# Four parts of layer 1's modulation computed beside layer 0's latent MLP, and two key weights split in the code ahead of a norm

## The chip, the cores and the metric

The kernel runs on one core of a Trainium2 chip. TensorE (PE in the profile) multiplies matrices, and its loads of stationary operands are listed as PEld; VectorE is DVE, ScalarE is ACT, GpSimd is POOL, and SP issues most of the DMAs. The metric is the device time of one launch in microseconds (us), the median of several runs.

## The reference

A backbone of two layers over 512 latent tokens and 256 context tokens, width 1024. Layer 0 mixes with mLSTM and RWKV heads, layer 1 with RG-LRU and neighbourhood attention; `ox` and `oc` below are the mixers' outputs. Each layer normalises, modulates, mixes, adds through a gate, and then does the same around a squared-ReLU MLP of width 4096. Shift, scale and gate of both halves of a layer are six vectors of 1024, the layer's *modulation*; they come from the conditioning vectors alone, so that they can be computed at any time before they are used.

```python
def ada_modulation(cond, w, b):
    m = jax.nn.silu(cond) @ w + b
    return jnp.split(m[:, None, :], 6, axis=-1)
...
    for layer in range(DEPTH):
        last = layer == DEPTH - 1
        sx1, cx1, gx1, sx2, cx2, gx2 = ada_modulation(c, ada_w[layer], ada_b[layer])
        sc1, cc1, gc1, sc2, cc2, gc2 = ada_modulation(c_ctx[None], ada_w[layer], ada_b[layer])
        nx = modulate(rms_norm(h_lat), sx1, cx1)
        nc = modulate(rms_norm(h_ctx), sc1, cc1)
...
        h_lat = h_lat + gx1 * ox
        h_lat = h_lat + gx2 * sq_relu_mlp(modulate(rms_norm(h_lat), sx2, cx2), mlp_w1[layer], mlp_w2[layer])
        if not last:
            h_ctx = h_ctx + gc1 * oc
            h_ctx = h_ctx + gc2 * sq_relu_mlp(modulate(rms_norm(h_ctx), sc2, cc2), mlp_w1[layer], mlp_w2[layer])
    return rms_norm(h_lat) * final_norm_w
```

## The kernel before

All matrix products go through the helper `mm` (L134), so most matmuls carry that line, and tiles tell them apart: `psg` is the output of a dense product, `psada` that of a modulation product. A scheduler under the program models each engine, and from the order in which the code asks for things and from its own costs it fixes the order of the instructions on each engine before the run. Every engine then works its own row in that order and waits at the first instruction whose operand is not there.

**A dense product** (`gemm`, L239) loads one weight block `w` by a DMA on SP, casts it on ScalarE to a rounded half `wh` (L232), subtracts it on VectorE or GpSimd to get the rest `wl` (L236), and runs 24 matmuls. `split_w` is the first part alone, `gemm_w` the second. After each product `gemm` adds a rate to a counter, and whenever the counter reaches one it takes one step of a *background* generator:

```python
        bg[2] += bg[1]
        while bg[2] >= 1.0:
            bg[2] -= 1.0
            next(bg[0], None)
```

**The background** is `ada` (L158), the modulation. One layer has six parts. A part is two *loads* of 2 MB (two DMAs of 1 MB each) into the one buffer `adaw` of its pool; each load feeds 16 program matmuls of 256 columns, which the trace lists as 32 records. After the second load come a copy to `rows` (L172), two transposes (L175) and four small VectorE instructions that write `mod` (L184). With one `adaw` buffer, a load is issued only after the matmuls of the load before it.

**Stages in time.** Up to about 355 us ("the heads stage") the kernel works off a string of letters (L1083): digits are steps of the four mLSTM heads of the context, `c` is a step of the RWKV input projection of the context, `a` starts the background, `R` ends the projection, drains the background and runs `pre(0, X)`, the preparation of the first RWKV step. `pre` stores a matrix to memory (`bkD`, L799), loads it back in another layout (L844), and the first RWKV matmul is `psA`. At the end of a head, the normalised head `hall` is made on GpSimd (L663, L673) and transposed by TensorE (L678); the RWKV projection has its own chain of small products (`psb`, `psw`, `psv`) for which VectorE, ScalarE and GpSimd work in turn. Up to about 985 us follow twelve RWKV steps with *fillers* (other work of layer 0) pulled between them by a table of counts; then the output projection of the latent tokens, and from about 1000 to 1366 us layer 0's latent MLP: four chunks, each of eight products into the hidden width and eight back, 64 in all, with `psg` of 128x512. Beside it run the background and, once, the norm of the context for layer 1 (`norm_mod` into `xhc`, `xlc`), which needs the shift and the scale, the first two parts of layer 1's modulation. Then come the norm of the latent tokens for layer 1 (`norm_mod(res, ...)`, whose last ScalarE step before the broadcast is `rs` at L310), the twelve key and value products of the context (`ukv`), and the rest of layer 1.

Of the kernel before, what the change touches and what calls it, by code (L numbers as in the profile page):

```python
# [21 lines left out]
CT = 256  # L22
# [95 lines left out]
def hybrid_kernel(ctx: ExitStack, tc: tile.TileContext, A, out):  # L118
    WS = [int(x) for x in "2222"]
    nc = tc.nc  # L120
# [37 lines left out]
    def ada(layer, parts, pa, psa, tag):  # L158
        for pair, half in parts:
            ps = psa.tile([P, 256], F32, tag=tag, name=nm("psada"))  # L160
            for k0 in range(0, NK, 4):

                w = pa.tile([P, 4, D], F32, tag="adaw", name=nm("adaw"))
                for i in range(0, 4, 2):
                    nc.sync.dma_start(w[:, i:i + 2, :], A["ada_w"][layer, pair, half, (k0 + i) // 2])
                for i in range(4):
                    k = k0 + i
                    for j in range(4):
                        mm(ps[32 * j:32 * j + 32, :], sc[:, k, :], w[:, i, 256 * j:256 * j + 256], k == 0, k == NK - 1)
                yield 1.8  # L170
            rows = pa.tile([P, 256], F32, tag="rows", name=nm("rows"), bufs=1)
            nc.vector.tensor_copy(rows, ps)  # L172
            pt = psa.tile([P, 2, P], F32, tag=tag, name=nm("pst"))
            for t in range(2):
                nc.tensor.transpose(pt[:, t, :], rows[:, P * t:P * t + P], ident)  # L175
            src = pt.rearrange("p t (i j r) -> p i t j r", i=2, j=2)
            for i, idx in enumerate(PAIRS[pair]):
                o = 8 * idx + 4 * half
                dst = mod[:, layer, o:o + 4, :].rearrange("p (j t) c -> p t j c", t=2)
                bo = COLS["ada_b"][0] + 48 * layer + o  # L180
                bias = cols[:, bo:bo + 4].rearrange("p (j t) -> p t j", t=2)
                one = 1.0 if idx in (1, 4) else 0.0
                for cnd in range(2):
                    nc.vector.scalar_tensor_tensor(dst[:, :, :, cnd], src[:, i, :, :, cnd], one, bias, op0=ALU.add, op1=ALU.add)  # L184
# [35 lines left out]
    bg = [iter(()), 0.0, 0.0]  # L220
# [18 lines left out]
    def gemm(ap, xs, psp, both=0, k0=0, k1=NK, x0=0):  # L239

        w = split_w(ap[:, P * k0:P * k1], both)
        res = [gemm_w(w, x, psp, x0) for x in xs]
# [4 lines that stand above are left out]
        return res  # L247
# [168 lines left out]
    psa1 = st_p1.enter_context(tc.tile_pool(name="psa1", bufs=1, space=PSUM, side="right"))  # L416
# [4 lines left out]
    with tc.tile_pool(name="pn", bufs=2) as pn, tc.tile_pool(name="pa0", bufs=16) as pa0:  # L421
# [11 lines left out]
        for q in range(4):  # L433
            ada_first(q, pa0, psa1, "ada")
            if q == 0:
                ws = [split_w(A["ev_in"][i], 2, pn) for i in range(2)]
# [33 lines left out]
    pa1 = st_a.enter_context(tc.tile_pool(name="pa1", bufs=1))  # L470
# [611 lines left out]
    work["c"] = rwkv_in(0, psg2, psm, "m")  # L1082
    for o in "0000a0c1ccc1cc11c1c22cc2c23c12ccc33cR33":  # L1083
        if o == "a":
            bg[:] = [itertools.chain(ada(0, ((1, 0), (1, 1), (2, 0), (2, 1)), pa1, psa1, "ada"),
                                     ada(1, ((0, 0), (0, 1), (1, 0), (1, 1)), pa1, psa1, "ada")), 0.5, 0.0]
        elif o == "R":
            for _ in itertools.chain(work["c"], bg[0]):
                pass
            bg[1] = 0  # L1090
            st_a.close()
            YA[0] = st_y.enter_context(tc.tile_pool(name="py", bufs=1)).tile([P, 4, 4, 64], F32, name="ya_c")
            pr = st_r.enter_context(tc.tile_pool(name="pr", bufs=1))
            add_set()
            banks.update(A=(psh2, "h", 1), I=(psa1, "ada", 1))
            S = sets[0].tile([P, 2, 4, 64], F32, tag="S", name="S0")
            nc.vector.memset(S, 0.0)
            X = new_x(0)
            nc.vector.memset(X[0:64], 0.0)
            pre(0, X)  # L1100
        else:
            next(work[o], None)
# [46 lines left out]
    ukv = plat.tile([P, 3, 4, CT], F32, name="ukv")  # L1149
# [3 lines left out]
    xhc = px1c.tile([P, NK, CT], F32R, name="xh1c")  # L1153
# [15 lines left out]
            pass  # L1169
        rb = stats.rms()  # L1170
    pa3 = st_3.enter_context(tc.tile_pool(name="pa3", bufs=1))
    bg[:] = [ada(1, ((2, 0), (2, 1)), pa3, psa3, "ada"), 0.25, 0.0]
    stats = Stats(LT, None, psa3, "st")
    for j, _ in enumerate(mlp(0, 0, LT, res, 8, psg3, "right", 0, rb, 2, stats)):
        if j == 8:
            with tc.tile_pool(name="pn1c", bufs=2) as pn:
                norm_mod(RES["c"], CT, 1, 1, 0, xhc, xlc, pn, stats_of(RES["c"], CT, pn, psg3).rms())
    for _ in bg[0]:
# [7 lines left out]
    xh = px.tile([P, NK, LT], F32R, name="xh1")  # L1186
    xl = px.tile([P, NK, LT], F32R, name="xl1")
    XL = [(xh, xl, LT)]
    with tc.tile_pool(name="pn1", bufs=2) as pn:
        norm_mod(res, LT, 0, 1, 0, xh, xl, pn, stats.rms(psg3, "g", work=pn))  # L1190
    for j, t0 in enumerate((0, 12, 16)):
        for i in range(4):
            ps, = gemm(A["od_in"][t0 + i], [(xhc, xlc, CT)], psg3, 2)
            nc.scalar.copy(ukv[:, j, i, :], ps)
    st_3.close()

    st_1 = ExitStack()
# [279 lines left out]
```

## Time and profile before

| | |
|---|---|
| time, median of 3 runs | 2068.69 us (2068.35 to 2078.05) |
| the profiled execution: its time | 2068.99 us |
| its span in the trace | 2067.1 us (1.9 us lie around it) |
| its mean granted TensorE clock | 0.971 of full speed |
| TensorE busy | 1959.7 us (95%) |
| VectorE, ScalarE, GpSimd busy | 1086.7 us (53%), 874.4 us (42%), 835.1 us (40%) |
| moved by DMA | 271.62 MB, 131 GB/s over the span |

TensorE is busy almost throughout, but its share is an average over stages: near full in the MLP and in most of the heads stage, lower at the end of the heads stage and in the RWKV steps. What an edit is worth therefore depends on the stage in which it takes or adds work.

### The profile page before, as it was taken

Reading aid. Unit: us, or ns where it says so; the run is one execution under the profiler, and the core shown is the slowest. Engines: PE = TensorE matmul, PEld = TensorE weight load, DVE = VectorE, ACT = ScalarE, POOL = GpSimd, SP = SyncE. Lnnn points to the kernel's source line nnn. Section 1 sums busy time; section 2 is a strip of 40 time slices with the busy share of each in tenths; the row PEclk is TensorE's granted clock in tenths of the full one; section 3 lists DMA queues with packets and bytes.
Section 4 is the critical chain, followed back from the end, with each engine's and each line's share of the span. In section 5 each row is a group of like instructions: output and inputs, shape, how many; then the busy total and the mean of one; then the engine's idle time right before and its main releaser. Section 6 shows DMA issues by size and latency. Waiting matters only on the chain. (4 is left out here: it accounts for less than half of the span.)

```text
span 2067.1 us, 36765 instructions
## 1 busy us (share of the span) xinstructions
PE 1959.7 (95%) x14924; PEld 1601.4 (77%) x14924; DVE 1086.7 (53%) x2087; ACT 874.4 (42%) x1441; POOL 835.1 (40%) x561
## 2 busy tenths in 40 slices
PE   6899999898887999999999999999999999999998
PEld 4788876776676899888787888887666687888887
DVE  6764555677878667766632221363656663122122
ACT  5444444354534444443433232343665743233232
POOL 1455554233432222224343444434545544444444
PEclk9999998898998999999999999999999999999999
DMA  8355557454585455553524232344120123322232
GB/s 322 96 202 207 192 207 246 107 153 108 165 247 156 123 172 158 149 138 123 209 97 133 92 100 94 94 127 127 51 62 29 59 67 93 100 92 92 93 98 74
DMA packets 171833, 271.62 MB, mean 131 GB/s; under 512 B 74960, under 2 KB 113488, under 8 KB 166544
## 3 DMA queue, kind: packets, MB, share of 16 engines
q1 hardware_dynamic: 166608, 263.76, 40.9%
q10 hardware_dynamic: 5056, 5.51, 0.8%
q8 instruction: 118, 1.93, 0.4%
q14 instruction: 51, 0.42, 0.1%
HBM read 244.06 MB, written 25.17 MB: 130 GB/s over the span
## 5 line engine op out<-in xcount | busy, mean ns | idle before, releaser
L236 POOL TENSOR_TENSOR wl<-w,wh 128x1024 fp32r<-128x1024 f32 (+3 forms) x252 | 573.5, 2279 | 861.0 <-PE psg L134 434.7
L232 ACT CAST wh<-w 128x1024 fp32r<-128x1024 f32 (+3 forms) x319 | 313.4, 985 | 529.0 <-PE psg L134 449.3
L134 PE MATMUL psg<-xh,wh 128*128 128x512 f32 (+1 forms) x1440 | 499.6, 362 | 13.6 <-DVE tm L884 6.1
L134 PE MATMUL psg<-xl,wh 128*128 128x512 f32 (+1 forms) x1440 | 498.9, 359 | 0.7 <-DVE xl L330 0.3
L134 PEld LDWEIGHTS psg<-xh,wh 128*128 128x128 f32 x1440 | 272.6, 191 | 69.6 <-issue 20.1
L134 PE MATMUL psg<-xh,wl 128*128 128x512 f32 (+1 forms) x1440 | 326.4, 357 | 0.0
L134 PEld LDWEIGHTS psg<-xl,wh 128*128 128x128 f32 x1440 | 274.6, 191 | 48.0 <-issue 7.4
L134 PEld LDWEIGHTS psg<-xh,wl 128*128 128x128 f32 x1440 | 242.1, 191 | 43.1 <-issue 7.0
L134 PE MATMUL psg<-hl,wh 128*128 128x512 f32 (+1 forms) x800 | 269.4, 351 | 0.9 <-DVE hl L276 0.9
L134 PE MATMUL psg<-hh,wh 128*128 128x512 f32 (+1 forms) x800 | 267.0, 350 | 0.6 <-DVE res_c L333 0.4
L333 DVE SCALAR_TENSOR_TENSOR res_l<-psg,mod,res_l 128x512 f32<-128x512 f32 (+1 forms) x108 | 74.1, 689 | 281.7 <-PE psg L134 281.7
L134 PEld LDWEIGHTS psg<-hl,wh 128*128 128x128 f32 x800 | 151.2, 189 | 22.5 <-DVE hl L276 1.3
L134 PEld LDWEIGHTS psg<-hh,wh 128*128 128x128 f32 x800 | 150.9, 189 | 22.7 <-issue 0.8
L134 PE MATMUL psg<-hh,wl 128*128 128x512 f32 (+1 forms) x800 | 166.1, 349 | 0.0
L378 DVE TENSOR_SCALAR r<-psg 128x512 f32<-128x512 f32 (+1 forms) x96 | 57.4, 600 | 179.2 <-PE psg L134 179.1
L134 PEld LDWEIGHTS psg<-hh,wl 128*128 128x128 f32 x800 | 131.6, 189 | 20.4
L276 DVE TENSOR_TENSOR hl<-r,hh 128x512 fp32r<-128x512 f32 (+1 forms) x96 | 90.7, 948 | 83.6 <-ACT hh L275 83.4
L379 ACT ACTIVATE r<-r 128x512 f32<-128x512 f32 (+1 forms) x96 | 53.5, 559 | 119.6 <-DVE r L378 119.5
L236 DVE TENSOR_TENSOR wl<-w,wh 128x1024 fp32r<-128x1024 f32 (+1 forms) x67 | 82.1, 1225 | 20.4 <-ACT wh L232 12.7
L884 DVE TENSOR_TENSOR tm<-M,Xi 64x15 f32<-64x15 f32 (+4 forms) x180 | 60.2, 335 | 23.9 <-DMA M<-dA 17.5
L134 PE MATMUL psada<-adaw,sc 128*32 128x256 f32 (+1 forms) x896 | 62.1, 381 | 9.0 <-DMA adaw<-in_ada_w_dram 5.1
L134 PE MATMUL psA<-ar,bk 64*128 64x128 f32 x384 | 55.8, 313 | 6.0 <-issue 3.1
(418 smaller groups left out, 2873.9 us busy)
## 6 DMA issues: line engine op xcount, KB each, us to landing
w<-in_w_dram SPq DMA_DIRECT2D x192, 512.0 KB, 3.6
adaw<-in_ada_w_dram SPq DMA_DIRECT2D x40, 1024.0 KB, 7.4
w<-in_ev_in_dram SPq DMA_DIRECT2D x47, 512.0 KB, 3.7
w<-in_od_in_dram SPq DMA_DIRECT2D x32, 512.0 KB, 3.6
adaw<-in_ada_dram SPq DMA_DIRECT2D x16, 512.0 KB, 11.3
w<-in_out_w_dram SPq DMA_DIRECT2D x32, 256.0 KB, 3.1
bk<-bkD SPq DMA_DIRECT2D x12, 512.0 KB, 4.0
ar<-arD SPq DMA_DIRECT2D x12, 512.0 KB, 5.0
```

What stands on the lines that cost most here:

```text
L134: return nc.tensor.matmul(o, l, r, start=start, stop=stop, skip_group_check=shared, **kw)
L232: nc.scalar.copy(wh, w)
L236: eng.tensor_tensor(wl, w, wh.bitcast(F32), op=ALU.subtract)
L276: nc.vector.tensor_tensor(l, x, h.bitcast(F32), op=ALU.subtract)
L333: nc.vector.scalar_tensor_tensor(r_, ps, modcol(layer, idx, m, cnd), r_, op0=ALU.mult, op1=ALU.add)
L378: nc.vector.tensor_scalar(r_, ps, 0.0, None, op0=ALU.max)
L379: nc.scalar.activation(r_, r_, AF.Square)
L884: nc.vector.tensor_tensor(t_, M[:, m:16, j:j + 1].to_broadcast([64, n, m]), Xi[:, j:j + 1, 0:m].to_broadcast([64, n, m]), op=ALU.mult)
```

## The change

Three places. In the heads stage the background holds only the last four parts of layer 0, at a rate of 0.34 steps a product instead of 0.5; the first four parts of layer 1, which followed there, are gone from it. Beside layer 0's latent MLP the background holds all six parts of layer 1 at 0.34 instead of the last two at 0.25, and the context norm of layer 1 comes after the 25th product rather than the 9th. The first two key weights of the context are split (`split_w`) in the code ahead of the latent norm instead of behind it. The number of modulation products is the same in total.

```diff
     for o in "0000a0c1ccc1cc11c1c22cc2c23c12ccc33cR33":
         if o == "a":
-            bg[:] = [itertools.chain(ada(0, ((1, 0), (1, 1), (2, 0), (2, 1)), pa1, psa1, "ada"),
-                                     ada(1, ((0, 0), (0, 1), (1, 0), (1, 1)), pa1, psa1, "ada")), 0.5, 0.0]
+            bg[:] = [ada(0, ((1, 0), (1, 1), (2, 0), (2, 1)), pa1, psa1, "ada"), 0.34, 0.0]
...
-    bg[:] = [ada(1, ((2, 0), (2, 1)), pa3, psa3, "ada"), 0.25, 0.0]
+    bg[:] = [ada(1, ((0, 0), (0, 1), (1, 0), (1, 1), (2, 0), (2, 1)), pa3, psa3, "ada"), 0.34, 0.0]
     stats = Stats(LT, None, psa3, "st")
     for j, _ in enumerate(mlp(0, 0, LT, res, 8, psg3, "right", 0, rb, 2, stats)):
-        if j == 8:
+        if j == 24:
             with tc.tile_pool(name="pn1c", bufs=2) as pn:
                 norm_mod(RES["c"], CT, 1, 1, 0, xhc, xlc, pn, stats_of(RES["c"], CT, pn, psg3).rms())
...
+    kv_c = [(j, i, t0 + i) for j, t0 in enumerate((0, 12, 16)) for i in range(4)]
+    ws = [split_w(A["od_in"][t], 2) for _, _, t in kv_c[:2]]
     with tc.tile_pool(name="pn1", bufs=2) as pn:
         norm_mod(res, LT, 0, 1, 0, xh, xl, pn, stats.rms(psg3, "g", work=pn))
-    for j, t0 in enumerate((0, 12, 16)):
-        for i in range(4):
-            ps, = gemm(A["od_in"][t0 + i], [(xhc, xlc, CT)], psg3, 2)
-            nc.scalar.copy(ukv[:, j, i, :], ps)
+    for n_, (j, i, t) in enumerate(kv_c):
+        ps = gemm_w(ws[n_], (xhc, xlc, CT), psg3) if n_ < len(ws) else gemm(A["od_in"][t], [(xhc, xlc, CT)], psg3, 2)[0]
+        nc.scalar.copy(ukv[:, j, i, :], ps)
```

What this does to the order on the engines is shown at three places. First TensorE at the end of the third mLSTM head, before: a context product `psg` ends there, then come the transposes of a modulation part, half a modulation load, the transposes of `hall` and the small RWKV products, with a second load between them.

```order
1052 L134 MATMUL psg_3369<-xh_89,wl_3367 128x256 x8
1053 L175 MATMUL pst_3438<-cst,rows_3436 128x128 x2
1054 L134 MATMUL psada_3445<-adaw_3446,sc 32x256 x16
1055 L678 MATMUL pst_2943<-cst,hall_2924 128x128 x2
1056 L678 MATMUL pst_2947<-cst,hall_2924 128x128 x4
1057 L134 MATMUL psb_3012<-q_3009,cst 128x256
```

```order
1064 L802 MATMUL psv_3123<-cst,v_2688 128x128 x2
1065 L134 MATMUL psg_3130<-sgd_1139,gup_2683 128x256
1066 L134 MATMUL psada_3445<-adaw_3557,sc 32x256 x8
1067 L134 MATMUL psw_3073<-low_1144,ul_3070 128x256
1068 L134 MATMUL psw_3078<-low_1146,ul_3070 128x256
1069 L134 MATMUL psada_3445<-adaw_3557,sc 32x256 x8
1070 L134 MATMUL psg_3411<-xh_89,wh_3407 128x256
```

The same place with the change: the head's last `psn` products now stand directly ahead of the transposes of `hall`, with only the two transposes of a modulation part between.

```order
1037 L134 MATMUL psg_3273<-xh_89,wl_3271 128x256 x8
1038 L134 MATMUL psn_2830<-vt_725,e_2711 128x129
...
1043 L134 MATMUL psn_2842<-cn_2835,kq_2150 128x129
1044 L175 MATMUL pst_3434<-cst,rows_3432 128x128 x2
1045 L678 MATMUL pst_2866<-cst,hall_2847 128x128 x2
1046 L678 MATMUL pst_2870<-cst,hall_2847 128x128 x4
1047 L134 MATMUL psb_2916<-q_2913,cst 128x256
```

The context product that stood behind the last `psn` stands ahead of it now, and both modulation loads are gone from between the small products.

Second TensorE in the latent MLP, between two products into the hidden width of its second chunk, before:

```order
3523 L134 MATMUL psg_12892<-xh_12036,wh_12888 128x512
3524 L134 MATMUL psg_12892<-xl_12037,wh_12888 128x512
3525 L134 MATMUL psg_12892<-xh_12036,wl_12890 128x512 x8
3526 L134 MATMUL psg_12928<-xh_12036,wh_12924 128x512
3527 L134 MATMUL psg_12928<-xl_12037,wh_12924 128x512
```

and with the change, where a whole load of the modulation stands between the products:

```order
3511 L134 MATMUL psg_12659<-xh_11844,wh_12655 128x512
3512 L134 MATMUL psg_12659<-xl_11845,wh_12655 128x512
3513 L134 MATMUL psg_12659<-xh_11844,wl_12657 128x512 x8
3514 L134 MATMUL psada_12556<-adaw_12684,sc 32x256 x16
3515 L134 MATMUL psg_12714<-xh_11844,wh_12710 128x512
```

Twelve such loads now lie in the MLP, where there were four.

Third ScalarE around the latent norm of layer 1, before (the casts of the first two key weights are those of `wh_14509` and `wh_14541`; `rs` is the norm's own step):

```order
971 L232 CAST wh_14509<-w_14507 128x1024
972 L298 ACTIVATE sq_14408<-res_l 128x512
973 L232 CAST wh_14541<-w_14539 128x1024
974 L298 ACTIVATE sq_14443<-res_l 128x512
975 L310 ACTIVATE rs_14466<-psst_12028,epsc 128x4
```

and with the change:

```order
968 L232 CAST wh_14465<-w_14463 128x1024
969 L298 ACTIVATE sq_14408<-res_l 128x512
970 L232 CAST wh_14471<-w_14469 128x1024
971 L298 ACTIVATE sq_14443<-res_l 128x512
972 L310 ACTIVATE rs_14478<-psst_11836,epsc 128x4
```

Only the numbers of the tiles differ: the two casts stood ahead of the norm's step before the change too.

## Rows read from the trace of the kernel before

**Rows 1.** The profile page: TensorE's busy tenths and granted clock in 40 equal slices.

```profile
PE   6899999898887999999999999999999999999998
...
PEclk9999998898998999999999999999999999999999
```

**Rows 2.** Windows by stage: start:end, length, busy us (records) of PE, PEld, DVE, ACT, POOL, granted clock.

```profile
100.00:300.00 200.00, 199.22 (x1487) 163.15 (x1491) 108.64 (x238) 85.64 (x172) 109.88 (x93) 1.00 0.57 199
...
310.00:320.00 10.00, 7.29 (x33) 4.76 (x34) 2.66 (x6) 3.32 (x7) 3.46 (x4) 0.54 0.69 230
320.00:330.00 10.00, 10.00 (x79) 6.89 (x79) 8.11 (x22) 7.11 (x17) 6.39 (x11) 0.78 0.98 324
...
420.00:680.00 260.00, 226.78 (x2725) 181.84 (x2724) 201.69 (x452) 121.16 (x223) 88.14 (x82) 0.89 0.58 162
...
1120.00:1360.00 240.00, 240.00 (x1061) 198.72 (x1060) 62.43 (x75) 77.64 (x94) 105.68 (x44) 1.00 0.31 97
```

**Rows 3.** Timeline of PE in the MLP: one burst of half a load, and the next product.

```profile
1015.52 1.07 PE L134 MATMUL psada<-adaw,sc 128*32 128x256 f32 x16
1016.52 0.74 PE L134 MATMUL psg<-xh,wh 128*128 128x512 f32 x2
```

**Rows 4.** Windows of the MLP, instructions on psg alone: with a load, without one.

```profile
1080.00:1100.00 20.00, 18.22 (x81) 14.77 (x80) 2.25 (x3) 0.00 (x0) 1.00 0.51 184
...
1120.00:1140.00 20.00, 20.00 (x89) 16.28 (x88) 2.77 (x4) 0.00 (x0) 1.00 0.27 79
```

**Rows 5.** Tile psada, 1000 to 1200 us: TensorE's idle time before it.

```profile
  issue: 2.8, 9
```

**Rows 6.** Tile adaw in the same stretch: its transfers.

```profile
DMA to landing us min/median/max: 5.0/6.1/7.2
```

**Rows 7.** Timeline of PE at the third head's end; idle before and releaser in brackets.

```profile
302.19 0.39 PE L134 MATMUL psn<-cn,kq 128*128 128x129 f32 x2
...
303.07 0.39 PE L134 MATMUL psg<-xh,wh 128*128 128x256 f32 x1
...
306.05 0.38 PE L175 MATMUL pst<-cst,rows 128*128 128x128 f32 x2
308.75 1.07 PE L134 MATMUL psada<-adaw,sc 128*32 128x256 f32 x16 [2.32 <-DMA adaw<-in_ada_w_dram]
311.91 1.93 PE L134 MATMUL psada<-adaw,sc 128*32 128x256 f32 x16 [2.08 <-DMA adaw<-in_ada_w_dram]
313.77 1.54 PE L678 MATMUL pst<-cst,hall 128*128 128x128 f32 x6
...
320.72 1.94 PE L134 MATMUL psada<-adaw,sc 128*32 128x256 f32 x16
...
324.87 0.39 PE L134 MATMUL psg<-xh,wh 128*128 128x256 f32 x1
```

**Rows 8.** Timeline of POOL there: the last step of `hall`.

```profile
310.16 1.47 POOL L673 TENSOR_TENSOR hall<-hall,rn 128x768 f32<-128x768 f32 x1 [0.58 <-DVE rn L672]
```

**Rows 9.** Timeline of SP's DMA issues during pre(0).

```profile
351.20 0.38 SPq L799 DMA_DIRECT2D bkD<-bk  x1
356.76 0.34 SPq L230 DMA_DIRECT2D w<-in_ev_in_dram  x1
358.61 0.33 SPq L844 DMA_DIRECT2D bk<-bkD  x1
```

**Rows 10.** Tile bkD, 300 to 400 us: its transfers.

```profile
DMA to landing us min/median/max: 3.7/3.9/4.2
```

**Rows 11.** Timeline of PE: the first RWKV matmul.

```profile
365.71 2.05 PE L134 MATMUL psA<-ar,bk 64*128 64x128 f32 x8 [3.09 <-issue]
```

**Rows 12.** Waits of PE, 355 to 1010 us: us in total, times, longest.

```profile
PE psI L134 <- DMA Xr<-invD: 7.3, 5, 3.9
PE psg L134 <- DVE tm L884: 6.1, 2, 4.4
```

**Rows 13.** Timeline of ACT around the latent norm of layer 1.

```profile
1363.91 1.05 ACT L232 CAST wh<-w 128x1024 fp32r<-128x1024 f32 x1 [2.19 <-PE psg L134]
...
1368.30 0.26 ACT L310 ACTIVATE rs<-psst,epsc 128x4 f32<-128x4 f32 x1 [1.14 <-PE psst L134]
```

**Rows 14.** Timeline of PE in the key and value products.

```profile
1399.76 0.58 PE L134 MATMUL psg<-xh1c,wh 128*128 128x256 f32 x1 [3.38 <-ACT wh L232]
```

## The prediction

> **What bounds the kernel now.** I read the page first: TensorE is near full in most slices, with a thinner patch from the eighth to the thirteenth, about 360 to 670 us [rows 1]. A share over the whole span prices no edit, so the windows by stage come next [rows 2]. In the heads stage, 100 to 300 us, TensorE is busy 199.2 of 200 us and VectorE only 108.6: work taken from TensorE there should shorten the stage. At 310 to 330 us it is thinner and its clock falls to 0.54 and 0.78, which is a stage of short dependent products. In the RWKV steps, 420 to 680 us, TensorE has 226.8 of 260 and VectorE 201.7: TensorE does not alone set the pace there. In the latent MLP, 1120 to 1360 us, TensorE is busy all 240 us at full clock: any work added there is paid in full. So the change takes TensorE work from a stage that is mostly TensorE's and puts the same work into one that is wholly TensorE's. If both were paid alike, nothing would come of it; the difference is what the sum has to find. The timelines of TensorE, GpSimd and SP at the seams of the heads stage follow, then the waits.
>
> **The MLP: eight more loads, four more parts.** One burst of half a load starts at 1015.52 and the next product at 1016.52, 1.0 us [rows 3], so a whole load takes 2.0. Windows of the product tile say the same from the other side: in 20 us without a load there are 89 records of it and 20.0 us, in 20 us with one load 81 records and 18.2 us [rows 4], so a load displaces 1.8 us. Eight loads are 14.4 to 16.0; take 15.4. Four parts also bring two transposes each; two start to the next instruction took at most a microsecond together, no row gives it alone, and I put the four parts at 1.1 in all. That is **+16.5**. Could it be less? Only if the loads fell into idle time, and the MLP has none: not below 14.4. More? Before the four loads that are there now TensorE idles 2.8 us in all under "issue" [rows 5], 0.7 a load; paid eight times that adds 5.6, so the upper bound is 22. The transfers don't enter: one lands in 5 to 7 us [rows 6], and the order places the bursts about every third product. Three products of 24 matmuls at 20 us for 89 records take 16 us, more than landing plus a burst, 9.2. Should that cover be gone, as with two bursts side by side, a load waits up to 7 us.
>
> **The context norm** moves from after the ninth to after the 25th product, with the same instructions on all engines and on both sides of it products of the same MLP: 0. What covers it is TensorE's queue of products. The background has done the shift and the scale by then (five steps at 0.34 are 15 products), so no wait replaces it; if it waited, TensorE would stand behind it, since its broadcast is in TensorE's row.
>
> **The key weights.** The code order moves, the row order doesn't: both casts stand ahead of the norm's step in both orders, and in the trace the second begins at 1363.91, the norm's step at 1368.30 [rows 13]. Nothing is removed and no DMA is moved: 0. The wait that is there, 3.38 us at 1399.76 for a cast [rows 14], belongs to a later weight, which is still split where it was.
>
> **The heads stage: what comes off.** TensorE's row loses eight loads. In time, four of them lie ahead of the end of the third head's `psn`; the rest lie at the seam and in `pre`. Along TensorE's row:
>
> 1. Up to the last `psn` of the third head: four loads at 2.0 are -8. But the order shows one context product moved from behind this `psn` to ahead of it; in the trace it takes from 303.07 to 306.05 [rows 7], +3. Together **-5**. Below this lies 0, if another engine sets the stage (the third rival), above it -8.
> 2. From that `psn` to the transposes of `hall`: 302.19 to 313.77, 11.6 us [rows 7], filled with the product, a modulation part and two bursts that wait 2.32 and 2.08 us for `adaw`. Without bursts the transposes go when `hall` is there. It starts its last step at 310.16 and takes 1.47, so it is there at 311.63 [rows 8], 9.4 after the `psn`. **-2.1**. The two DMA waits are thus not worth their 4.4: the chain through GpSimd is next. If that chain too became faster by an emptier GpSimd, up to -4.4.
> 3. From the first burst among the small products to the next context product, 320.72 to 324.87, 4.15 us [rows 7], there is one load at low clock between small products that wait for other engines. **-2**; bounds 0 (the small products were what was late) and -4.15.
> 4. To the first RWKV matmul. The store of `bkD` is issued at 351.20 and lands 3.9 later [rows 10], at 355.1. The load of `bk` is issued only at 358.61, because SP's queue stands behind a weight load at 356.76 [rows 9], which itself waits for a buffer that TensorE frees late. The order now has the `bk` load directly behind the store. -3.5 on `psA`, which starts at 365.71 [rows 11]. Bounds: 0, if `psA`'s "issue" wait of 3.09 is for something else, and -5.8, if the bursts that lay ahead of the store add 2.3. Take **-3.5**.
>
> The sum is -12.6, with bounds from 0 to about -22.
>
> **The RWKV steps.** Nothing is edited, but with an earlier start the fillers, transfers and steps meet otherwise. TensorE waits there in pieces: 7.3 us in five for a transfer, 6.1 in two for VectorE [rows 12]. One or two such pieces more or less are -8 to +8; I take **0**.
>
> **The sum.** 16.5 - 12.6 + 0 = +3.9 on the profiled execution's 2068.99 (span 2067.1 and 1.9 around it): 2072.9. That execution is 0.3 above the median of the runs, 2068.69, so 2072.6; rounded, **2072**.
>
> **A rule against the row.** TensorE's row in the MLP reads 240.00 of 240 us, and its weight loads 198.7, 83% [rows 2]. By the record counts a load displaces eight or nine products [rows 4], which says that the added matmuls find no gap. The Trainium skill, "Perfetto Trace Analysis", section "Identifying the Most-Contended Engine", says that matmul occupancy is a bad measure of how near TensorE is to its limit and that the share of weight-load time should be read. By that rule the MLP would have 17% room and the added loads could be free, 2056 in all. The row on displaced products speaks against it.
>
> **The rivals.**
>
> *A. The sum as above*, between 2064 and 2079: 0.57.
>
> *B. The heads stage gives back more than it held.* All eight loads come off the end (-16), the DMA waits too (-4.4), and TensorE keeps its clock through the seam: at 310 to 330 us it lost 0.46 and 0.22 of ten microseconds [rows 2], -6.8. Together -27 against +16.5: 2058. For it speaks that TensorE was full from 100 to 300. Against: `hall` is ready only 9.4 us after the head, so the seam stays thin. 0.18, spread around 2058.
>
> *C. The other side: the heads stage is set by chains.* mLSTM steps and the small RWKV products go from engine to engine; the background's bursts then only fill TensorE's waiting time, and a full-looking row is full because of them. Place: terms 1 to 3; price: they give nothing, term 4 perhaps 2. That is +14.5, 2083. It decides once less than about 6 us come off the stage. For it speaks the seam, where two waits of 4.4 us hide a chain that ends only 2.1 us earlier [rows 7, 8]; against it that VectorE is only 54% busy from 100 to 300 us [rows 2]. 0.11.
>
> *D. The clock falls for longer.* The seam now holds about 9 us of nearly empty TensorE in one piece, where bursts stood between. At 310 to 320 us, behind two idle pieces, the granted clock was 0.54 of full speed [rows 2], so almost throughout 1.2 of the two levels of 1.2 and 2.4 GHz. If it falls earlier and returns later, the price of that stretch is paid once more, +6.8: 2079 to 2080. 0.08. The Trainium skill, "TensorE: Matmul & The Clock Gate", section "HAM oscillation — how this bites in real kernels", says that waits between groups of matmuls throttle the clock again for the group behind; the row of 0.54 agrees.
>
> *E. The added work is free, or the key weights do come earlier.* If the MLP takes the loads at nothing, -12.6: 2056; if the split removes the 3.38 us, 2069. Displaced records and the unchanged order speak against: 0.06, nearly all for the first.
>
> That the change doesn't do what it says, that is, that the key split changes nothing, is part of A.
>
> **How the numbers follow.** About 0.5%, 10.3 us, is what a measurement of this kernel can tell from no change: 2058.3 to 2079.0. A lies within it but for its rim; B lies on its lower edge, and with E gives most of the faster share; C and D give the slower one. Faster 0.23, within 0.58, slower 0.19. The range leaves out the half of B and E that lies lowest and most of C: 2056 to 2082. A's own range is 2064 to 2079.
>
> **What would show it.** In the trace of the changed kernel: `psada` records in the MLP 384 instead of 128, and the MLP from its first to its last product about 16 us longer at full clock, with no wait for `adaw`. `psn` of the third head ends near 297; `hall`'s transposes 9 to 10 us later; `psA` near 353 instead of 365.7. The same idle of about 3 us in the key and value products. Wrong would be the prediction if `psA` came less than 6 us earlier (C), if the RWKV steps gained or lost over 8 us between `psA` and the MLP's start, or if the MLP grew by less than 14 us (E) or by over 22.

## The result: slower, by 0.3 to 0.6% in three groups of runs

The changed kernel takes 2084.12 us (median of 6 runs, 2079.31 to 2086.73), the kernel before 2071.11 (6 runs, 2066.55 to 2078.05). The ratio is 1.0063, with a 95% interval from 1.0046 to 1.0081. That is 13 us more, where the sum said 3.9 (3.3 as rounded to 2072), and it lies above the range. In later groups of runs the same program came out at 1.0029 (1.0012 to 1.0047), and without its third edit, which leaves the order on every engine as it is, at 1.0046 (1.0030 to 1.0062). The profiled execution of the change has a span of 2077.4 us, 10.3 more than that of before.

First the two rows of the page that answer to [rows 1].

```profile
PE   6899989898888999999999999999999999999998
...
PEclk9999998999988999999999999999999999999999
```

They hardly differ; such a page can't say where 10 us went. The windows that answer to [rows 2] (columns as there) say a little more: the seam at 310 to 320 us is emptier and slower, and in the MLP there are 1206 records instead of 1061 in the same time, since each of the added ones is small.

```profile
100.00:300.00 200.00, 199.50 (x1440) 167.17 (x1439) 112.47 (x233) 87.30 (x180) 113.86 (x96) 1.00 0.47 160
310.00:320.00 10.00, 7.60 (x25) 5.42 (x24) 6.81 (x14) 6.73 (x16) 5.41 (x8) 0.50 0.37 117
320.00:330.00 10.00, 9.78 (x63) 8.77 (x63) 7.21 (x17) 7.43 (x15) 3.83 (x7) 0.91 0.54 154
420.00:680.00 260.00, 224.28 (x2802) 182.52 (x2801) 200.11 (x459) 123.52 (x230) 84.35 (x81) 0.89 0.59 164
1120.00:1360.00 240.00, 239.45 (x1206) 193.04 (x1203) 66.13 (x103) 74.82 (x96) 97.63 (x42) 1.00 0.42 143
```

What does tell is a list of landmarks: the start of the same instruction in both traces. The first RWKV matmul is the first `psA`; "first" and "last product" are the first and last start of `psC<-X,Q`, the output product of the RWKV steps; the latent norm is its first VectorE instruction at L327; then the first key product of the context. The table gives the stretches between them, for the kernel before, for two more executions with its rows (e18 and e1 below; e1 differs from before only behind the latent norm), and for four executions of the rows of the change (e2, below, has them up to the latent norm).

| kernel | to first `psA` | to first product | to last product | to latent norm | MLP, to first key product | rest | span |
|---|---|---|---|---|---|---|---|
| before | 365.7 | 82.4 | 491.5 | 63.5 | 367.3 | 696.7 | 2067.1 |
| e18, the rows of before | 365.6 | 81.6 | 495.8 | 63.5 | 367.4 | 697.7 | 2071.6 |
| e1, the rows of before up to the MLP | 366.6 | 82.1 | 496.0 | 63.4 | 385.1 | 695.5 | 2088.7 |
| the change | 350.5 | 88.0 | 495.8 | 60.3 | 384.8 | 698.0 | 2077.4 |
| e3, its rows | 350.5 | 90.0 | 496.0 | 60.9 | 384.6 | 698.3 | 2080.3 |
| e10, its rows | 349.9 | 89.2 | 496.1 | 60.5 | 384.5 | 698.1 | 2078.3 |
| e2, its rows up to the MLP | 350.8 | 89.2 | 500.0 | 60.9 | 365.8 | 696.0 | 2062.7 |

Read down a column: the same rows give the same times again to within 2.3 us, but for the long stretch to the last product, where they differ by up to 4.5. The heads stage gives 15.2 us to the first `psA`, the MLP costs 17.5, and about 6 to 8 us of the lead are gone by the first product, in a stretch where nothing was edited. The 491.5 of before is the lowest of its column: the profiled execution of before was some 4 us quicker there than e18 and e1 with the same rows, so the pair of profiles overstates the loss in the steps by that.

The seam of the heads stage after, which answers to [rows 7] (timeline of TensorE), [rows 8] (GpSimd), [rows 9] (SP) and [rows 11]:

```profile
299.79 0.39 PE L134 MATMUL psn<-cn,kq 128*128 128x129 f32 x2
300.01 0.38 PE L175 MATMUL pst<-cst,rows 128*128 128x128 f32 x2
309.44 1.54 PE L678 MATMUL pst<-cst,hall 128*128 128x128 f32 x6 [9.04 <-POOL hall L673]
...
318.77 0.55 PE L134 MATMUL psg<-xh,wh 128*128 128x256 f32 x1 [1.60 <-DVE k L705]
```

```profile
307.91 1.47 POOL L673 TENSOR_TENSOR hall<-hall,rn 128x768 f32<-128x768 f32 x1 [4.62 <-DVE rn L672]
```

```profile
342.51 0.36 SPq L799 DMA_DIRECT2D bkD<-bk  x1
344.94 0.33 SPq L844 DMA_DIRECT2D bk<-bkD  x1
```

```profile
350.52 0.79 PE L134 MATMUL psA<-ar,bk 64*128 64x128 f32 x5
```

The wait for `adaw` is replaced by one of 9.04 us for `hall`, and TensorE is at half clock behind it (0.50 from 310 to 320 us). The load of `bk` follows its store after 2.4 us, where it took 7.4.

In the MLP the tile view of `psada` (900 to 1300 us; answers to [rows 5]) lists 384 records; the "issue" in it is idle time of the weight loads' row (PEld), and of TensorE it lists none. The key and value products (timeline of TensorE; [rows 14]) wait as before:

```profile
L134 PE MATMUL psada<-adaw,sc x384: 379/379/634, 994.5 to 1233.0; 128*32 128x256 f32 x192
...
  issue: 6.0, 18
```

```profile
1408.95 0.38 PE L134 MATMUL psg<-xh1c,wh 128*128 128x256 f32 x1 [3.10 <-ACT wh L232]
1412.17 2.17 PE L134 MATMUL psg<-xh1c,wl 128*128 128x256 f32 x16 [1.07 <-DVE wl L236]
```

### The profile page after: what moved, and what is told of

It is laid out like the page before. It is cut to its first block, busy times and chain, and to the rows that moved or that the text cites. A ratio compares the mean times of both kernels' runs of the same rounds, so it can differ in the third digit from the quotient of the medians.

```text
span 2077.4 us, 36764 instructions
## 1 busy us (share of the span) xinstructions
PE 1957.6 (94%) x14924; PEld 1602.2 (77%) x14924; DVE 1080.1 (52%) x2087; ACT 871.4 (42%) x1439; POOL 831.5 (40%) x561
## 5 line engine op out<-in xcount | busy, mean ns | idle before, releaser
L236 POOL TENSOR_TENSOR wl<-w,wh 128x1024 fp32r<-128x1024 f32 (+3 forms) x252 | 572.4, 2274 | 889.4 <-PE psg L134 493.1
L276 DVE TENSOR_TENSOR hl<-r,hh 128x512 fp32r<-128x512 f32 (+1 forms) x96 | 86.0, 899 | 79.2 <-ACT hh L275 79.2
L236 DVE TENSOR_TENSOR wl<-w,wh 128x1024 fp32r<-128x1024 f32 (+1 forms) x67 | 80.7, 1205 | 29.6 <-ACT wh L232 18.0
L884 DVE TENSOR_TENSOR tm<-M,Xi 64x15 f32<-64x15 f32 (+4 forms) x180 | 50.1, 279 | 23.0 <-DMA M<-dA 19.9
L886 DVE TENSOR_TENSOR Xi<-Xi,tm 64x15 f32<-64x15 f32 (+4 forms) x180 | 54.7, 304 | 4.0
```

Source lines behind the costliest of these rows:

```text
L236: eng.tensor_tensor(wl, w, wh.bitcast(F32), op=ALU.subtract)
L276: nc.vector.tensor_tensor(l, x, h.bitcast(F32), op=ALU.subtract)
L884: nc.vector.tensor_tensor(t_, M[:, m:16, j:j + 1].to_broadcast([64, n, m]), Xi[:, j:j + 1, 0:m].to_broadcast([64, n, m]), op=ALU.mult)
L886: nc.vector.tensor_tensor(Xi[:, m:16, 0:m], Xi[:, m:16, 0:m], t_, op=ALU.add)
```

## The experiments

Each group has its own runs of before beside it (medians 2072.3, 2077.3, 2075.6, 2076.0 and 2078.1 us), and ratios are taken within a group.

**What each part is worth (e1 to e4).** e1 takes only the MLP's part of the change, e2 only the heads' part, e3 all but the key weights, and e4 is the change at the old rate.

```diff
 e1 (from before)
-    bg[:] = [ada(1, ((2, 0), (2, 1)), pa3, psa3, "ada"), 0.25, 0.0]
+    bg[:] = [ada(1, ((0, 0), (0, 1), (1, 0), (1, 1), (2, 0), (2, 1)), pa3, psa3, "ada"), 0.34, 0.0]
...
-        if j == 8:
+        if j == 24:
 e2 (from before)
+    nc.vector.memset(mod[:, 1], 0.0)
...
-            bg[:] = [itertools.chain(ada(0, ((1, 0), (1, 1), (2, 0), (2, 1)), pa1, psa1, "ada"),
-                                     ada(1, ((0, 0), (0, 1), (1, 0), (1, 1)), pa1, psa1, "ada")), 0.5, 0.0]
+            bg[:] = [ada(0, ((1, 0), (1, 1), (2, 0), (2, 1)), pa1, psa1, "ada"), 0.34, 0.0]
 e3 (from the change): the third edit taken back
 e4 (from the change)
-            bg[:] = [ada(0, ((1, 0), (1, 1), (2, 0), (2, 1)), pa1, psa1, "ada"), 0.34, 0.0]
+            bg[:] = [ada(0, ((1, 0), (1, 1), (2, 0), (2, 1)), pa1, psa1, "ada"), 0.5, 0.0]
```

> The heads stage of before, with its eight parts; beside the latent MLP all six parts of layer 1 and the context norm after the 25th product, so that four parts of layer 1 are computed twice. Everything ahead of the MLP should stand where it stood. Theory 1 (the MLP pays its loads in full, and the heads' gain is partly lost in the RWKV steps): +17 to +18 us on before. Rival 2 (the MLP's price is larger than the trace shows, and the heads' gain is kept whole): +23 or more. Rival E of the prediction (the loads are free): 0.

Measured: 2089.82 us, ratio 1.0084 (1.0059 to 1.0108), +17 us; its MLP takes 385.1 us. The loads are paid in full, at 2.2 us each with all that their parts bring along.

> The heads stage of the change (four parts at 0.34), the rest as before; the first four parts of layer 1's modulation are left out and set to zero. Theory 1: the first RWKV matmul about 15 us earlier, the output projection about 10 earlier, -8 to -10 us in all. Rival 2 (the lead is kept): -14 to -16. If the heads stage were set by chains of other engines: 0 to -4.

Measured: 2064.29, ratio 0.9956 (0.9938 to 0.9974), -9 us, although the first `psA` comes 14.9 us earlier. As theory 1 says, part of the lead is lost before the MLP. With e1 that makes +8, which lies among the +13, +9.5 and +6 measured for the change.

> The change with the key weights split where they were split before. The order of the engines' rows is that of the change but for tile numbers, so all theories say: no difference from the change, +12 us on before within 3 us.

Measured: 2082.40, ratio 1.0046 (1.0030 to 1.0062), +9.5. No difference to the change that the intervals could tell.

> The change with the background of the heads stage at 0.5 steps a product instead of 0.34: the same eight loads, done earlier. Theory 1 (steps lose lead because they have a chain of their own): the same as the change within 3 us, lead at the first RWKV matmul 13 to 16 us, at the output projection about 10. Rival 3 (what the steps take depends on where the work happens to meet, and a shift of a few instructions is worth several us either way): the lead at the end of the steps differs by more than 4 us from the change's, in either direction.

Measured: 2076.43, ratio 1.0020 (1.0002 to 1.0038), +4. The stretch to the first product takes 82.8 us, as before and not as in the change; to the last product it is 496.2, no difference. The same work, done somewhat earlier in the heads, costs about 6 us less than in e3. That fits theory 3, but the sign that was named for it is not there: the latent norm comes at 995.2 us, against 994.6, 997.4 and 995.7 in the change, e3 and e10, and much of what the profiled execution gains lies behind the MLP (694.6 for 698.0).

**Where the lead goes (e5 to e8).** The waits of TensorE in the change from the first `psA` to the first product (us in total, times, longest) name VectorE twice, with its serial inverse (`tm`, `Xi`):

```profile
PE psg L134 <- DVE tm L884: 4.1, 1, 4.1
PE psA L134 <- DVE Q L858: 3.5, 3, 1.8
PE psg L134 <- DVE Xi L886: 3.4, 1, 3.4
```

VectorE's row there, in the change (first) and before, shows what `psg` waits for. It is not the inverse itself but the read-out of a product (L704, L705), which frees its buffer. In the change it stands behind `wl` and a long `tm`; before it stands behind a `wl` too, but ahead of the long `tm`.

```profile
385.00 1.50 DVE L886 TENSOR_TENSOR Xi<-Xi,tm 64x60 f32<-64x60 f32 x1
386.43 1.21 DVE L236 TENSOR_TENSOR wl<-w,wh 128x1024 fp32r<-128x1024 f32 x1
387.56 2.34 DVE L884 TENSOR_TENSOR tm<-M,Xi 64x55 f32<-64x55 f32 x1
389.83 0.73 DVE L704 SCALAR_TENSOR_TENSOR zs<-psg,der,zs 128x511 f32<-128x511 f32 x1
...
390.61 0.73 DVE L705 SCALAR_TENSOR_TENSOR zs<-psg,der,zs 128x511 f32<-128x511 f32 x1
```

```profile
397.27 1.21 DVE L236 TENSOR_TENSOR wl<-w,wh 128x1024 fp32r<-128x1024 f32 x1
...
399.39 0.73 DVE L704 SCALAR_TENSOR_TENSOR zs<-psg,der,zs 128x511 f32<-128x511 f32 x1
...
400.27 0.70 DVE L705 SCALAR_TENSOR_TENSOR zs<-psg,der,zs 128x511 f32<-128x511 f32 x1
...
402.51 2.46 DVE L884 TENSOR_TENSOR tm<-M,Xi 64x64 f32<-64x64 f32 x1
```

TensorE in the change starts again when that read-out ends:

```profile
391.49 0.76 PE L134 MATMUL psg<-xh,wh 128*128 128x512 f32 x1 [4.14 <-DVE tm L884]
```

e5 is the change at a rate of 0.42; e6 moves the other way; e7 and e8 shorten the inverse of step 0 in before and in the change.

```diff
 e5 (from the change)
-            bg[:] = [ada(0, ((1, 0), (1, 1), (2, 0), (2, 1)), pa1, psa1, "ada"), 0.34, 0.0]
+            bg[:] = [ada(0, ((1, 0), (1, 1), (2, 0), (2, 1)), pa1, psa1, "ada"), 0.42, 0.0]
 e6 (from before)
-                                     ada(1, ((0, 0), (0, 1), (1, 0), (1, 1)), pa1, psa1, "ada")), 0.5, 0.0]
+                                     ada(1, ((0, 0), (0, 1), (1, 0), (1, 1), (2, 0), (2, 1)), pa1, psa1, "ada")), 0.62, 0.0]
...
-    bg[:] = [ada(1, ((2, 0), (2, 1)), pa3, psa3, "ada"), 0.25, 0.0]
+    bg[:] = [iter(()), 0.0, 0.0]
 e7 (from before), e8 (from the change)
-        for j in range(15):
+        for j in range(15 if s else 1):
```

> The change with the heads' background at 0.42. The stretch from the first RWKV matmul to the first state product of step 0 took 82.4 us before, 88.0 in the change and 82.8 at a rate of 0.5. Theory 3 (the loss there comes from the order that the shifted rows happen to take): 82 to 84 or 88 to 90, one of the two, with the total 4 or 11 us above before accordingly. Theory 1 (any lead gained in the heads is partly lost there): 86 or more, 9 to 13 us above before.

Measured: 2096.51, ratio 1.0083 (1.0056 to 1.0111), +17. The stretch to the first product is 90.2, as in the change; but the next one, to the last product, takes 514.3 instead of 496. Neither theory had that. The profiled execution was the slowest of six (2084.30 to 2102.92), so that the 514.3 stands for the slow end of this kernel.

> The other direction: from before, the last two parts of layer 1 move into the heads stage too (ten parts at 0.62), and the latent MLP has no background. Eight loads in the MLP cost 17.5 us, so four fewer save 8.7 there; eight loads in the heads cost 15.2 us to the first RWKV matmul and 9 in all, so four more cost 4.5 to 7.6. Expected: 1 to 4 us faster than before. If the seam of the heads takes them badly: 3 us slower.

Measured: 2081.82, ratio 1.0022 (1.0006 to 1.0038), +4.5. The MLP falls by 8.9 us as expected, but the first `psA` comes 18.7 later, and though the first product follows sooner (78.5 us) the stretch to the last takes 507.8: the seam takes more loads badly.

> Before, with 28 of the 30 small VectorE instructions of the inverse left out for step 0 alone. In before, TensorE waits 4.4 us for them once. If these waits are what differs, the stretch from the first RWKV matmul to the first state product of step 0 falls from 82.4 by 4 to 8 us.

> The change, with the same 28 instructions left out for step 0. In the change TensorE waits for them twice, 3.4 and 4.1 us, and then runs at half clock. If the collision of these with the read-out of the product buffers on VectorE is the cause, the stretch falls from 88.0 to within 2 us of the same kernel of before; if it is not, it stays 5 us or more longer.

Measured: 71.4 us for the stretch in e7 and 80.8 in e8, each some 7 to 11 less than with the whole inverse, but still 9.4 apart. The inverse is not what makes the difference; this guess failed. The later stretch grows to 516.9 and 505.9, and each has one run (2083.25 and 2085.70), so that the totals say nothing.

**One place by hand, and half of the move (e9 to e12).** The scheduler takes an ordering edge without a wait; `after(a, b)` puts `a` behind `b` in the row of their engine. `inv0` holds the `tm` instructions of step 0.

```diff
 e9 (from the change)
...
+                if si == 1 and i == 2:
+                    after(inv0[9], rd)
 e11 (from before)
-                                     ada(1, ((0, 0), (0, 1), (1, 0), (1, 1)), pa1, psa1, "ada")), 0.5, 0.0]
+                                     ada(1, ((0, 0), (0, 1)), pa1, psa1, "ada")), 0.5, 0.0]
...
-    bg[:] = [ada(1, ((2, 0), (2, 1)), pa3, psa3, "ada"), 0.25, 0.0]
+    bg[:] = [ada(1, ((1, 0), (1, 1), (2, 0), (2, 1)), pa3, psa3, "ada"), 0.25, 0.0]
 e12 (from before; rd is L704 here, L705 in e9)
...
+                if si == 1 and i == 2:
+                    after(rd, inv0[10])
```

> The change, with one place of VectorE's row put by hand as it stands in before and at a rate of 0.5: the read-out of the third product of the latent projection stands ahead of the long end of the inverse for step 0, where the change has it behind. Nothing else is edited. Theory 3 in its sharper form (the lead is lost because TensorE waits about 4 us for this read-out, which frees a product buffer, and then runs at half clock): the stretch from the first RWKV matmul to the first state product of step 0 falls from 88 to 90 to 83 to 85, and the total by 4 to 7 us. Theory 1 (a loss by the steps' own chain): no change of either.

Measured: 2091.45, ratio 1.0074 (1.0052 to 1.0096). The long wait is gone, and the stretch falls from between 88 and 90 to 86.0, less than expected: other waits stand in its place, as the waits of TensorE in that stretch show. And the next stretch takes 504.1 instead of 496. One place put right made the whole slower, by 10 us against e10 of the same group.

```profile
PE psg L134 <- DVE Xi L891: 3.4, 1, 3.4
PE psbc L134 <- ACT rx L742: 2.5, 1, 2.5
...
PE pst L679 <- POOL hall L674: 1.6, 1, 1.6
```

> The change itself once more, beside the others of this group: 8 to 14 us above before; the stretch to the first state product of step 0 88 to 90 us, the latent MLP 384 to 386.

Measured: 2081.81, ratio 1.0029 (1.0012 to 1.0047), +6, less than the 8 to 14 expected; its stretches, as expected, stand in the table above.

> Half of the move: from before, two of the four parts of layer 1 (four loads) go to the latent MLP, at the old rates of 0.5 and 0.25. In the MLP four loads cost 8.7 us. In the heads stage the last four of the 16 loads stand at the seam, which is where terms 2 to 4 of the prediction lie (-7.6) beside their own matmuls at the third head (-5): -5 to -9 there and then up to 6 lost again or not, by the row order. Expected 0 to 5 us above before; a version that beats before only if the seam gives all of it.

Measured: 2091.24, ratio 1.0067 (1.0043 to 1.0090), +14, where 0 to 5 were expected. Lead of 11.8 us at the first `psA`, MLP +10.5, but 508.3 us from the first to the last product.

> Before, with the read-out of that third product put behind the long end of the inverse, as the change has it (by some more places than there). Theory 3: the stretch from the first RWKV matmul to the first state product grows from 82.4 to 86 or more, with a second wait of TensorE of 3 to 6 us for VectorE there. Theory 1: it stays at 82 to 83.

Measured: the second wait is there, but the stretch is 83.4, one more than before. The added wait (same view) is mostly given back ahead of the first product: the waits for `X` fall from 2.5 to 0.6 us, one of 2.0 for `rx` is gone.

```profile
PE psg L134 <- DVE tm L887: 9.3, 2, 5.4
```

So single waits don't add up to the stretch, and that left the whole order as the thing to test. From the first to the last product these kernels took 491 to 517 us, but not all of that is order: e5 and e11 have the same rows there and took 514.3 and 508.3, e2 and the change 500.0 and 495.8.

**The whole order (e13 to e18).** From the preparation of the first RWKV step to the latent MLP every instruction that the kernel issues outside `ada` is noted in the order of the code, which is the same in all these kernels. The rows of before (or, for e14, of the change) are then laid on as a chain of ordering edges on each engine. `ROWS` holds them as lists of numbers; no instruction is added or taken away, and `ada` stays free. The two sets of rows differ widely: of VectorE's 1102 instructions only 484 follow the same one in both, of TensorE's 4990 it is 4559.

```diff
+    q_ = _ar.array("h", _zl.decompress(_b64.b85decode(ROWS)))
+    while q_:
+        n_ = q_[0]
+        for x_, y_ in zip(q_[1:n_], q_[2:n_ + 1]):
+            after(rec[y_][1], rec[x_][1])
+        q_ = q_[n_ + 1:]
```

> The change, with the rows of all five engines from the preparation of the first RWKV step to the latent MLP held in the order that they have in before (order alone; no instruction differs). Order theory: the stretch from the first RWKV matmul to the last state product, 584 to 586 us in the change, falls to the 574 to 578 of before; with the lead of 15 us and the MLP's 17.5 the total comes to +1 to +5 us on before. Chain theory: the stretch stays at 583 or more, the total at +8 to +13.

> Before, with the same rows held in the order of the change. Order theory: the stretch grows from 574 to 578 to 583 to 588 us, the total by 6 to 11 us. Chain theory: no difference from before within 3 us.

> The change at a rate of 0.42, whose stretch took 604.5 us, with the rows of before from the first preparation on. Order theory: 574 to 580 us. Chain theory: 595 or more.

> Half of the move (two parts of layer 1 in the MLP), with the rows of before from the first preparation on. Order theory: lead of 11.8 us at the first RWKV matmul, +10.5 in the MLP, the stretch 574 to 578: -3 to +1 us on before, the best candidate among these. Chain theory: the stretch 590 or more and +10 us or more in all.

> The change, with VectorE's row alone held in the order of before from the first RWKV preparation on; the scheduler orders the other engines afresh around it. If VectorE's order is what carries the loss: the stretch from the first RWKV matmul to the last state product 570 to 578 us, total -4 to +4 us on before. If the rows of several engines count together: 580 us or more, and +5 us or more.

> Before, with its own rows held on all engines: a control. No difference from before, within 4 us, and the stretch at 574 to 578. If holding rows gains by itself, 5 us or more faster, and what the held change gained must be reduced by that.

Measured:

| kernel | us | ratio (95%) | to first `psA` | to first product | to last product | MLP |
|---|---|---|---|---|---|---|
| e13, the change, rows of before | 2072.75 | 0.9988 (0.9970 to 1.0005) | 353.9 | 78.3 | 493.1 | 385.1 |
| e14, before, rows of the change | 2108.36 | 1.0156 (1.0131 to 1.0182) | 395.2 | 89.1 | 499.2 | 366.8 |
| e15, rate 0.42, rows of before | 2077.59 (one run) | | 354.3 | 78.5 | 498.7 | 385.1 |
| e16, half way, rows of before | 2074.17 | 0.9988 (0.9972 to 1.0003) | 356.8 | 80.7 | 502.4 | 376.2 |
| e17, the change, VectorE's row alone | 2084.81 | 1.0041 (1.0024 to 1.0059) | 348.5 | 87.6 | 504.9 | 385.1 |
| e18, before, its own rows | 2077.86 | 1.0008 (0.9988 to 1.0027) | 365.6 | 81.6 | 495.8 | 367.4 |

With the rows of before the change reaches the first product at 432.2 us, against 447 to 449 with the same rows in before and 438.5 to 440.5 with its own: a lead of 15 to 16.5 us stands there, and the loss in the total is gone. The interval of e13 lies apart from those of e10 and e3, and that of e16 from that of e11. Holding rows gains nothing by itself (e18). Between the first `psA` and the last product the same rows take 27 us out of e5 (604.5, in its slowest execution, to 577.2) and 14 out of e11 (597.3 to 583.1). Not all came as expected: e13 is 3.5 us better than the best that was named, e16 has the total that was expected but 583.1 us for the stretch instead of 574 to 578. The rows of the change put into before cost 32 us instead of 6 to 11, but in the profiled execution 29.5 are lost ahead of the first `psA`, where sixteen loads don't fit between rows that were laid for eight; its waits of TensorE from 280 to 396 us begin with

```profile
PE psada L198 <- DMA adaw<-in_ada_w_dram: 16.3, 7, 5.1
```

In the steps e14 loses some 7 us in the stretch to the first product, as expected. VectorE's row alone (e17) does not do it: +8.5 us, and 592.5 from the first `psA` to the last product. The windows of the stretch to the first product and of the next, in the change (first) and in e13 (second), show the same number of TensorE records to within 13. In the first of the two stretches TensorE is idle 13.8 us in the change and 9.6 in e13, and busy 74.2 and 68.7, at a clock of 0.86 and 0.93: about half of what the order costs there are waits, the rest the lower clock. In e3 and e10 (third and fourth), with the rows of the change, TensorE is idle 11.1 and 13.3 us and busy 78.9 and 75.9, at 0.80 and 0.84: there the lower clock takes the larger part. In the later stretch the clock differs with the same rows, too: e16 (last) is 9.3 us longer there than e13, of which 3.2 are idle time and 6.1 busy time, at 0.92 instead of 0.94.

```profile
350.50:438.50 88.00, 74.16 (x604) 60.88 (x606) 58.82 (x129) 37.88 (x71) 30.26 (x29) 0.86 0.39 109
438.50:934.30 495.80, 450.59 (x6264) 395.63 (x6261) 357.04 (x853) 225.54 (x399) 141.19 (x109) 0.95 0.57 157
```

```profile
353.90:432.20 78.30, 68.72 (x600) 55.23 (x602) 56.37 (x121) 39.28 (x74) 28.41 (x29) 0.93 0.47 122
432.20:925.30 493.10, 452.56 (x6251) 397.69 (x6247) 361.97 (x853) 223.80 (x395) 141.34 (x107) 0.94 0.57 157
```

```profile
350.50:440.50 90.00, 78.86 (x606) 64.51 (x606) 58.38 (x129) 38.18 (x71) 29.15 (x29) 0.80 0.39 107
```

```profile
349.90:439.10 89.20, 75.92 (x605) 62.53 (x607) 58.79 (x129) 37.92 (x71) 30.00 (x29) 0.84 0.39 107
```

```profile
437.50:939.90 502.40, 458.70 (x6252) 401.75 (x6247) 361.19 (x853) 223.23 (x395) 140.44 (x107) 0.92 0.56 154
```

No version beats before by more than the measurement can tell: e13 and e16 come to -2.5 us, with 1 inside both intervals.

## Why the prediction was wrong, step by step

- **The MLP, +16.5.** Right in kind and nearly in size: 367.3 to 384.8, +17.5, and 384.5 to 385.1 us in every kernel with the six parts there. TensorE's idle time in that stretch is the same, 1.8 us before and 1.9 after, so the loads are paid as busy time, 2.2 us each. The upper bound of 22 rested on a misreading: the 2.8 us under "issue" [rows 5] are not TensorE's but those of the row of weight loads (PEld), since the view of a tile mixes the engines; of TensorE alone it lists none. Rival E is refuted by e1, and with it the rule that the prediction set against the row: weight loads at 83% left no room for the eight loads.
- **The heads stage, -12.6.** -15.2 at the first `psA`. Term 1 was too large: the third head's last `psn` moved from 302.19 to 299.79, -2.4 and not -5. Term 2 was right: 9.65 us from there to the transposes of `hall`, -1.9 for -2.1. Term 3 was right: 11.1 to 9.3 us from those to the next context product, -1.8 for -2. Term 4 was too small, beyond its bound of -5.8: from that product to the first `psA` it is 31.75 us instead of 40.84, -9.1 for -3.5. The `bk` load was freed as said (TensorE's idle time falls by 2.9 us), but two loads, the bursts between 333 and 352 us, came off the path as well (its busy time falls by 6.2, some 4 of it the bursts). That the stage came near the forecast is luck in part, since terms 1 and 4 are off in opposite directions. Rival C is refuted. Rival D's half clock is there (0.50), yet the stage came out quicker; a lower clock that costs time shows behind it, in the stretch to the first product (0.80 to 0.86 with the rows of the change, 0.89 to 0.93 with those of before).
- **The context norm, 0, and the key weights, 0.** Right. e3 doesn't differ from the change, and the rest of the kernel takes 698.0 for 696.7, within the spread of the other executions (694.6 to 698.3, but for 691.6 in e6).
- **The RWKV steps, 0, with bounds of 8 either way.** This is the step that failed. From the first `psA` to the latent norm they took 637.4 us before and 644.1 in the change: +6.7, inside the bounds but not 0, and +3 to +6 for the change, e3 and e10 against e18 and e1. With the rows of before held, the change takes 634.6. "With an earlier start the fillers, transfers and steps meet otherwise" was the right sentence with the wrong cause: the rows do not merely meet otherwise, they are ordered otherwise by the scheduler, and the new order costs 6 to 8 us up to the first product. Up to the latent norm, 3 of them come back. The order was there to be read ahead of the run; the prediction used it for the seam, the MLP and the latent norm alone, and priced a new order of some 7,000 instructions at nothing.
- **The sum.** In the two profiled executions the terms read +17.5 for the MLP, -15.2 for the heads stage, +6.7 for the steps and +1.3 behind the first key product: +10.3, where the sum said 16.5 - 12.6 + 0 = +3.9. With the rows of before held, the change measures -2.5 us (-6 to +1); with its own rows it is +6 to +13 over three groups, and by the spans of the table +6 to +9 against e18, so that the +13 of the first six runs is at the upper end. The range missed it by 2 us; the median of before itself rose by 2.4 us with its second three runs, so chance has a part in falling just outside.

Open stays which places of the new order cost the time, and why the later stretch takes 496 to 500 us with the rows of the change and 508 to 514 with those of e5 and e11. e7, e8, e9 and e12 show only that it is no single one of the places tried. VectorE's row alone is not enough (e17); which of the other engines' rows matter beside it was not tried.

## What to carry to other kernels

Where a scheduler orders the rows, an edit in one stage can re-order the next, and that can cost a good part of what the edit brings (here 6 to 8 of 15 us by the first product): compare the rows of every stage behind the edit, not only of the edited one. To measure the edit alone, hold the old order behind it, with the old kernel under its own held order as a control. And a move of background work brings only the difference of two prices: the same eight loads cost 2.2 us each in a full MLP, and taking them out of the heads stage gave 1.9 each at the first `psA`, of which the new order left 1.1 in the total (e2).

## What the runs showed of the hardware

VectorE instructions of the inverse take about 0.2 us, but now and then up to 2.5 (2.34 at 387.56 in the change, 2.46 at 402.51 before). In the traces of before and the change 41 of 720 took over 0.9 us; beside each of them GpSimd runs an instruction with two operands, mostly a weight split of 128x1024, and both end within 0.1 us of each other. Beside the two named above it is this:

```profile
386.38 3.45 POOL L236 TENSOR_TENSOR wl<-w,wh 128x1024 fp32r<-128x1024 f32 x1
```

```profile
402.50 2.40 POOL L236 TENSOR_TENSOR wl<-w,wh 128x1024 fp32r<-128x1024 f32 x1 [0.60 <-issue]
```

So each of these 41 ended only with the GpSimd instruction beside it; the cause was not tested. And runs of one kernel, with one order of rows, differ, and the granted clock with them: e5 took from 2084.30 us at a mean clock of 0.971 to 2102.92 at 0.960. A stretch read from one execution of each of two kernels therefore mixes order and clock, and only a difference that comes again in several executions, as that up to the first product does, can be put down to order.
